# The closing of a nearest-neighbour upsampling kernel: GpSimd in place of SyncE waits for the last transfers, with both closing barriers gathered ahead of that wait

## The chip, the cores and the metric

The kernel runs on one core of one Trainium2 chip. The time is the device time of one execution in microseconds (us). So the time follows that last update, and what comes after the span counts in it. All runs quoted are at a granted clock of 1.0.

Names: VectorE (DVE), ScalarE (ACT), GpSimd (POOL), TensorE (PE) and SyncE (SP) are the five engines. The traces list each engine's waits and semaphore updates under its own queue (SPq, POOLq), called its sequencer here. A semaphore stands in them as a count that instructions and transfers change and on which instructions wait. A transfer counts its landing on one in sixteen increments (256 landing updates for the 16 transfers, in the trace before). "The landing" below means the sixteenth increment of the last store. The "span" runs from the first to the last instruction of the program. The "runtime's close" is the name here for what comes after it, seen only by its semaphore updates.

## The reference

```python
def setup_inputs():
    return {'x': np.random.randn(16, 64, 64, 64).astype(np.float32), 'scale_factor': 2}

def reference(x, scale_factor):
    # ... result[:, :, i, j] = x[:, :, i // scale_factor, j // scale_factor]
```

A pure copy: 16.78 MB are read and each element is written four times, 67.11 MB.

## The kernel before

Four loads of 4 MB bring the input into one large tile. VectorE and ScalarE expand pieces of it (9/16 and 7/16 of the rows), and SyncE issues twelve stores. The first eight are of 4 MB and the last four of 8 MB.

```python
def store(part, r0, k, at):
    # ... kv = k * 9 // 16; u is a piece of the big tile, seen as rows to be expanded
    nc.vector.tensor_copy(out=u[:, :kv], in_=expanded(xp[:, r0 : r0 + kv, :]))
    nc.scalar.copy(out=u[:, kv:], in_=expanded(xp[:, r0 + kv : r0 + k, :]))
    # ...
    nc.sync.dma_start(out=dst[:, r0 : r0 + k, :], in_=u)
# ...
for n, (q, r0) in enumerate(small):
    store(q, r0, 32, WX + n % 2 * (WU // 2))
for n, (q, r0) in enumerate(large):
    store(q, r0, 64, (0, WX)[n % 2])
```

The change concerns what the framework puts behind this. It stands in no line of the kernel; the profile puts it down to one line, L138 before, called the closing line here. It gathers the engines at two barriers, 0 and 1: each engine reports its arrival to GpSimd, which releases all when they have come. As built, the closing block is this (my shortening; "arrive" is a DRAIN that adds 1 to the gather semaphore, "pass" waits for the release semaphore and takes 1 off it):

```
SyncE:                       wait for the 8 semaphores of all 16 transfers and for both copy engines
                             (5 event-semaphore instructions and a DRAIN), then
                             arrive 0, pass 0, arrive 1, pass 1
ScalarE, VectorE, TensorE:   arrive 0, pass 0, arrive 1, pass 1
GpSimd:                      DRAIN d0, gather 0 (wait for 4 arrivals), release 0 (+4),
                             DRAIN d1, clear (semaphores 99 to 108 to zero), DRAIN d2,
                             gather 1, release 1
```

Of the kernel before, what the change touches and what calls it, by code (L numbers as in the profile page):

```python
# [1 line left out]

# [4 lines left out]



EARLY = 1  # L10


def begin_before_barrier(nc):



    blocks = nc.main_func.blocks
    main, body = blocks[0], blocks[1]
    sp = mybir.EngineType.SP
    loads = [i for i in body.instructions if i.engine == sp][:EARLY]  # L20
    for load in loads:
        assert isinstance(load, mybir.InstDMACopy), type(load)
        assert not (load.sync_info and load.sync_info.on_wait)
    names = [i.name for i in loads]
    body.instructions = [i for i in body.instructions if i.name not in names]
    kept = list(main.instructions)
    at = next(
        n
        for n, i in enumerate(kept)
        if i.engine == sp and isinstance(i, mybir.InstDrain)  # L30
    )
    kept[at:at] = loads
    main.instructions = kept


@with_exitstack
def kernel(
    ctx: ExitStack,
    tc: tile.TileContext,
    x: bass.AP,  # L40
    scale_factor: int,
    out: bass.AP,
):
    nc = tc.nc
    nc.at_finalize(begin_before_barrier)
    P = nc.NUM_PARTITIONS
    s = int(scale_factor)
    B, C, H, W = x.shape
    R = B * C * H
    fdt = x.dtype  # L50



    WX = R // P * W
    WU = 16384
    mem_pool = ctx.enter_context(tc.tile_pool(name="mem", bufs=1))
    mem = mem_pool.tile([P, WX + WU], fdt, name="mem")



    M4 = R // (4 * P)
    blocks = [(1, M4, 0), (1, M4, 2), (1, M4, 3), (4, M4 // 4, 1)]
    WB = M4 * W
    assert M4 * P * 4 == R and 2 * WB == WU

    xf = x.rearrange("b c h w -> (b c h) w")
    of = out.rearrange("b c (h hd) w -> (b c h) (hd w)", hd=s)

    parts = []
    for n, (j, m, slot) in enumerate(blocks):  # L70
        first = n * P * M4
        xt = mem[:, slot * WB : (slot + 1) * WB].rearrange(
            "p (j m w) -> p j m w", j=j, m=m
        )
        nc.sync.dma_start(
            out=xt.rearrange("p j m w -> p j (m w)"),
            in_=xf[first : first + P * M4, :].rearrange(
                "(j p m) w -> p j (m w)", j=j, p=P
            ),
        )  # L80
        parts.append([(xt[:, jj], first + jj * P * m, m) for jj in range(j)])

    def expanded(rows):
        return rows.unsqueeze(2).unsqueeze(4).to_broadcast(
            [P, rows.shape[1], s, W, s]
        )

    def store(part, r0, k, at):

        xp, first, m = part  # L90
        kv = k * 9 // 16
        u = mem[:, at : at + k * s * W * s].rearrange(
            "p (k a w b) -> p k a w b", k=k, a=s, w=W
        )
        nc.vector.tensor_copy(out=u[:, :kv], in_=expanded(xp[:, r0 : r0 + kv, :]))  # L95
        nc.scalar.copy(out=u[:, kv:], in_=expanded(xp[:, r0 + kv : r0 + k, :]))  # L96
        dst = of[first : first + P * m, :].rearrange("(p m) w -> p m w", p=P)
        nc.sync.dma_start(out=dst[:, r0 : r0 + k, :], in_=u)



    small = [(q, r0) for n in (0, 3) for q in parts[n] for r0 in range(0, q[2], 32)]
    large = [(q, r0) for n in (1, 2) for q in parts[n] for r0 in range(0, q[2], 64)]
# [6 lines that stand above are left out]
# [1 line left out]
_INS = ['x', 'scale_factor']  # L111
_OUTS = [((16, 64, 128, 128), 'float32')]

_NUMBERS = {'scale_factor': 2}


# [26 lines left out]
```

## Time and profile before

| | before |
|---|---|
| time, median of 3 runs | 199.46 us (199.43 to 199.73) |
| span of the profiled execution | 197.712 us |
| share of the 16 DMA engines in use | 98.9% |
| VectorE, ScalarE busy | 20%, 26% |
| last store issued / landed | 164.576 / 196.899 us |
| landing to end of span | 0.813 us |
| end of span to last semaphore update of the runtime's close | 1.907 us |

From the profile page of the kernel before, the busy shares, the DMA queue's line and the chain of waits:

```profile
DVE 40.2 (20%) x12; ACT 51.3 (26%) x13; POOL 0.2 (0%) x4
q1 hardware_dynamic: 2688, 83.89, 98.9%
DMA 69%; ACT 14%; issue 0%; ACTq 0%
```

The transfers fill the whole span (98.9%). No change in the waits at the end can move that part. What follows the last landing is invisible in these shares, because semaphore instructions are not counted as busy. It has to be read from the closing line's own instructions.

The view of the closing line's instructions, kernel before. The columns are: line, engine's queue, operation, count, shortest/median/longest duration in ns, first and last start in us:

```profile
L138 SPq EVENT_SEMAPHORE  x7: 17/28/28, 165.0 to 197.7; - x7
L138 POOLq EVENT_SEMAPHORE  x4: 17/17/17, 197.1 to 197.6; - x4
L138 POOLq DRAIN  x3: 34/41/70, 0.8 to 197.5; - x3
L138 SPq DRAIN  x3: 7/7/7, 197.0 to 197.3; - x3
L138 PEldq EVENT_SEMAPHORE  x2: 51/51/51, 197.2 to 197.7; - x2
L138 POOLq EVENT_SEMAPHORE_RANGE_CLEAR  x1: 93/93/93, 197.3 to 197.3; - x1
```

All four gathers and releases of GpSimd lie at 197.1 us or later, and so does the clear. Its first DRAIN, d0, ran at 0.8 us. Whom SyncE's queue waited for (total us, times, longest):

```profile
SPq L138 <- DMA out_dram<-mem: 31.8, 2, 19.3
```

The trace's instruction records resolve the tail to the nanosecond (start, duration in ns; the passes of ScalarE and VectorE and the arrivals are left out; S97 is the release semaphore, S96 the gather):

```
196.899      sixteenth increment of the last store (S108)
196.916  28  SyncE   wait S108, S102 ends
196.981   7  SyncE   DRAIN (last of the waits)
197.039   7  SyncE   DRAIN, arrive 0
197.071  17  GpSimd  gather 0
197.149  17  GpSimd  release 0
197.230  70  GpSimd  DRAIN
197.329  93  GpSimd  clear
197.451  34  GpSimd  DRAIN
197.529  17  GpSimd  gather 1
197.607  17  GpSimd  release 1
197.661  51  TensorE pass 1        -> span ends 197.712
```

Each of these starts after the one above it, so all 0.813 us are on the critical path, although they are 0.4% of the time.

### The profile page before, as it was taken

The page shows a single profiled execution, that of the slowest core. Times are in us where ns is not written, and L with a number is a line of the kernel's source. Part 1 is how long each engine was busy: PE and PEld are TensorE (multiplying, and loading weights), DVE is VectorE, ACT ScalarE, POOL GpSimd, SP SyncE. Part 2 cuts the span into 40 slices and gives each one's busy share as a digit, 9 for nine tenths or more (in the row PEclk, how much of TensorE's full clock was granted, in tenths as well). Part 3 has the DMA queues.
Part 4 walks back from the last instruction along what each step waited for, and adds up shares of the span by engine and source line. Part 5 has one row for each costly group of instructions (what it writes and reads, how often), then busy time and mean ns, then how long its engine had stood idle before and what let it go on. Part 6 is the DMA issues. An engine that isn't in the chain of part 4 may idle for free.

```text
span 197.7 us, 116 instructions
## 1 busy us (share of the span) xinstructions
DVE 40.2 (20%) x12; ACT 51.3 (26%) x13; POOL 0.2 (0%) x4
## 2 busy tenths in 40 slices
DVE  0055000000405059505050007200810090000000
ACT  2057000000415150606069207400830092000000
POOL 0000000000000000000000000000000000000000
DMA  8999999999999999999999999999999999999994
GB/s 318 424 424 424 438 464 383 424 413 424 424 424 424 444 444 451 451 424 438 424 424 424 424 424 424 464 477 491 451 451 424 424 424 424 424 424 424 424 424 212
DMA packets 2688, 83.89 MB, mean 424 GB/s; under 512 B 256, under 2 KB 256, under 8 KB 256
## 3 DMA queue, kind: packets, MB, share of 16 engines
q1 hardware_dynamic: 2688, 83.89, 98.9%
HBM read 16.78 MB, written 67.11 MB: 424 GB/s over the span
## 4 chain that ended last, share of the span: by engine, by line
DMA 69%; ACT 14%; issue 0%; ACTq 0%
DMA out_dram<-mem 63%; ACT mem L96 14%; DMA mem<-in_x_dram 6%; ACTq L96 0%
## 5 line engine op out<-in xcount | busy, mean ns | idle before, releaser
L96 ACT COPY mem<-mem 128x3584 f32<-128x3584 f32 (+1 forms) x12 | 50.0, 4174 | 112.5 <-DMA out_dram<-mem 102.2
L95 DVE COPY mem<-mem 128x4608 f32<-128x4608 f32 (+1 forms) x12 | 40.2, 3359 | 123.1 <-DMA out_dram<-mem 110.8
L96 ACT ACT_TABLE_LOAD x1 | 1.3, 1283 | 0.8 <-PEq L124 0.8
L124 POOL MEMSET const-bfloat16-1.0<- 128x1 bf16 x1 | 0.1, 102 | 0.0
L124 POOL MEMSET const-uint8-127<- 128x1 uint8 x1 | 0.1, 102 | 0.0
L124 POOL MEMSET const-float32-0.0<- 128x1 f32 x1 | 0.1, 99 | 0.2 <-issue 0.2
L124 POOL MEMSET const-float32-1.0<- 128x1 f32 x1 | 0.1, 99 | 0.0
## 6 DMA issues: line engine op xcount, KB each, us to landing
out_dram<-mem SPq DMA_DIRECT2D x8, 4096.0 KB, 16.1
mem<-in_x_dram SPq DMA_DIRECT2D x4, 4096.0 KB, 25.8
out_dram<-mem SPq DMA_DIRECT2D x4, 32.3
```

Source lines behind the costliest of these rows:

```text
L95: nc.vector.tensor_copy(out=u[:, :kv], in_=expanded(xp[:, r0 : r0 + kv, :]))
L96: nc.scalar.copy(out=u[:, kv:], in_=expanded(xp[:, r0 + kv : r0 + k, :]))
L124: nc = _bacc.Bacc("TRN2", target_bir_lowering=False, num_devices=1)
```

## The change

Its intent: do all closing work that does not need the data while the last transfer is still under way. GpSimd, which has to perform the clear and the release anyway, waits for the transfers itself, so that no hand-over from SyncE is left behind the landing. Both gathers and the first release move ahead of that wait. The waits are sorted so that the last store's semaphore is the last to be waited for. The diff without its assertions:

```diff
+def close_on_gpsimd(nc):
+    # ...  last = semaphore of the last store; mine = GpSimd's instructions of the closing block
+    wait = end[0]                       # SyncE's DRAIN with all the waits
+    waits = sorted(wait.sync_info.on_wait, key=lambda w: w.id != last)
+    d0, gather0, release0, d1, clear, d2, gather1, release1 = mine
+    landed = mybir.InstDrain(
+        name=wait.name, engine=pool, debug=wait.debug,
+        sync_info=mybir.SyncInfo(on_wait=waits, on_update=[]),
+    )
+    others = [i for i in end if i.engine != pool and i is not wait]
+    blocks[-1].instructions = others + [
+        d0, gather0, release0, gather1, d1, landed, clear, d2, release1
+    ]
 # ...
     nc.at_finalize(begin_before_barrier)
+    nc.at_finalize(close_on_gpsimd)
```

Putting `last` first in the list looks odd. The waits stand in five event-semaphore instructions, with one wait left on the DRAIN itself, which executes last. In the changed kernel that one is S108, the first of the sorted list. In the kernel before, whose list is not sorted, it is S101 (196.981), and the last store's semaphore (S108) stands in the last of the five event-semaphore instructions (196.916), with one DRAIN behind it.

More of the change, by code (lines that the diff above doesn't have):

```diff
@@ L33, in begin_before_barrier @@
     main.instructions = kept
+def close_on_gpsimd(nc):
+    blocks = nc.main_func.blocks
+    sp, pool = mybir.EngineType.SP, mybir.EngineType.Pool
+    stores = [
+        i
+        for i in blocks[1].instructions
+        if i.engine == sp and isinstance(i, mybir.InstDMACopy)
+    ]
+    last = stores[-1].sync_info.on_update[0].id
+    end = list(blocks[-1].instructions)
+    wait = end[0]
+    assert wait.engine == sp and isinstance(wait, mybir.InstDrain)
+    waits = sorted(wait.sync_info.on_wait, key=lambda w: w.id != last)
+    assert waits[0].id == last and len(waits) > 2
+    mine = [i for i in end if i.engine == pool]
+    kinds = [type(i).__name__ for i in mine]
+    assert kinds == [
+        "InstDrain",
+        "InstEventSemaphore",
+        "InstEventSemaphore",
+        "InstDrain",
+        "InstISA",
+        "InstDrain",
+        "InstEventSemaphore",
+        "InstEventSemaphore",
+    ], kinds
+    d0, gather0, release0, d1, clear, d2, gather1, release1 = mine
+    landed = mybir.InstDrain(
+        name=wait.name,
+        engine=pool,
+        debug=wait.debug,
+        sync_info=mybir.SyncInfo(on_wait=waits, on_update=[]),
[3 more added lines that the diff above has]
+        d0, gather0, release0, gather1, d1, landed, clear, d2, release1
+    ]
 @with_exitstack
```

## The prediction

> **What bounds the kernel now.** The kernel moves 83.89 MB (16.78 read, 67.11 written) and the page's queue table gives the transfers 98.9% of 16 engines' span; VectorE and ScalarE are busy 20% and 26%. The chain of waits puts 69% on DMA and 14% on ScalarE's copies, the last transfer being a 32 us store issued at 164.58 us. The change touches none of that. It only touches what follows the last landing.
>
> **The tail before** (the trace's instruction records and semaphore updates; the view of the closing line's instructions gives their first and last starts and durations). The sixteenth increment of the last store comes at 196.899 us. SyncE's wait ends 17 ns later (196.916); its closing DRAINs start at 196.981 and 197.039. GpSimd, the gatherer, then runs in series: gather 197.071, release 197.149, DRAIN 197.230, semaphore clear 197.329 (93 ns), DRAIN 197.451, gather 197.529, release 197.607. The last engine (PE) passes at 197.661 and takes 51 ns: span 197.712. So 0.81 us lies between the last landing and the end of the span, all of it on the critical path.
>
> **What the change does.** The order of instructions shows the compute and transfer parts identical. In the closing block all four other engines arrive at both barriers, and GpSimd does gather 0, release 0, gather 1 and a DRAIN, as soon as the last store is issued (about 165 to 165.5 us), under the 32 us transfer: free. The early landings are waited for there too; the last store's own semaphore is put by the lowering on the final DRAIN, so nothing but that one wait is left to end when the data lands. After it there is: DRAIN, clear, DRAIN, release, and the engines' pass. Number of instructions: unchanged.
>
> **Cost, with before's own steps.** Wake 17 ns (as SyncE; GpSimd woke from its gather 25 ns after its last increment, so the same size), DRAIN to clear 99, clear to DRAIN 122, DRAIN to the next instruction 78, release to PE's pass 54, pass 51: 0.42 us after landing in place of 0.81. [...] Saved: 0.39 us (SyncE's two DRAINs and hand-over 0.155; first gather and release, 0.159; second gather 0.078). All of it is critical, since nothing runs beside it.
>
> **What lies outside the span.** 199.46 - 197.71 = 1.75 us. After the span the semaphore updates go on to 199.62 us[...]. It starts from the same last release in both kernels, so I expect it to shift whole. It might gain or lose 0.1 to 0.2 us because four engines now stand at their last wait for 32 us.
>
> **Prediction.** 199.46 - 0.39 = 199.07 us, that is 0.2% faster; range 198.85 to 199.28 (the three runs before spread over 0.30). Chance of faster by over 2%: 0.005; within 2%: 0.99; slower by over 2%: 0.005.
>
> **What would show each step.** Span of about 197.3 us; the closing line's SyncE records with no wait for a landing; GpSimd's gathers near 165 us; the clear about 0.12 us after the last landing and the final release about 0.32 after; last store's issue still near 164.6 and its landing near 196.9; DMA share still 99%. Wrong if: GpSimd wakes from a landing clearly later than SyncE; the clear takes longer right after the wait; a gather is still found after the landing; the transfers' own time changes; or the runtime's close takes up the gain because an engine other than the releasing one limits it (then the span falls by 0.39 and the time by less).

The steps, each from the start of one record to the start of the next in the trace before, are 17 + 99 + 122 + 78 + 54 + 51 = 421 ns left after the landing; of 813 ns that saves 0.392 us, and 199.46 - 0.39 = 199.07 us. In "What lies outside the span", "it" is what follows the span; that it would shift whole, and the 0.1 to 0.2 us allowed for, were guesses.

## The result, and the profile after

| | before | changed |
|---|---|---|
| median time, same rounds | 199.56 us (6 runs) | 199.08 us (6 runs; 198.94 to 199.31) |
| span of the profiled execution | 197.712 | 197.279 |
| last store issued / landed | 164.576 / 196.899 | 164.547 / 196.902 |
| landing to end of span | 0.813 | 0.377 |
| end of span to last update of the close | 1.907 | 1.905 |

The ratio is 0.9977, with a 95% interval of 0.9964 to 0.9990. Ratios and intervals are those of the record, from the fast runs of the same rounds; they are not quite the ratio of the medians, nor always that of the plain means (0.9994 in e2, where the record has 0.9997). The kernel is faster by 0.2%, well inside "same" at the 2% mark.

From the profile page of the changed kernel, the same three lines; they show no change in the body beyond 0.2 points of DMA share:

```profile
DVE 40.2 (20%) x12; ACT 51.3 (26%) x13; POOL 0.2 (0%) x4
q1 hardware_dynamic: 2688, 83.89, 99.1%
DMA 69%; ACT 14%; issue 0%; ACTq 0%
```

The closing line's instructions in the changed kernel (columns as before):

```profile
L183 POOLq EVENT_SEMAPHORE  x9: 17/17/43, 165.1 to 197.2; - x9
L183 POOLq DRAIN  x4: 34/38/70, 0.8 to 197.1; - x4
L183 SPq DRAIN  x2: 7/68/128, 164.9 to 165.3; - x2
L183 SPq EVENT_SEMAPHORE  x2: 17/17/17, 165.2 to 197.2; - x2
L183 PEldq EVENT_SEMAPHORE  x2: 51/51/51, 165.2 to 197.2; - x2
L183 POOLq EVENT_SEMAPHORE_RANGE_CLEAR  x1: 93/93/93, 197.0 to 197.0; - x1
```

GpSimd now has nine event-semaphore instructions in place of four, five of them the waits that SyncE had; the first starts at 165.1 us. SyncE's DRAINs are over by 165.3 us. In SyncE's waits the landing is gone from the closing line; what it waits for there is the barrier (the profile puts it down to another engine's queue, PE's):

```profile
SPq L183 <- PEq L183: 32.1, 2, 31.9
```

The tail in the changed kernel's instruction records:

```
165.084  17  GpSimd  gather 0
165.163  17  GpSimd  release 0
165.412  17  GpSimd  gather 1
165.493  70  GpSimd  DRAIN
   ...
196.902      sixteenth increment of the last store (S108)
196.925  34  GpSimd  DRAIN, wait S108 ends
196.989  93  GpSimd  clear
197.110  34  GpSimd  DRAIN
197.174  17  GpSimd  release 1
197.228  51  TensorE pass 1        -> span ends 197.279
```

Start to start the steps are 23 + 64 + 121 + 64 + 54 + 51 = 377 ns. Before they were 17 + 65 + 58 + 32 + 78 + 81 + 99 + 122 + 78 + 78 + 54 + 51 = 813 ns. The difference, 0.436 us, is the gain. By these steps SyncE's arrival and the hand-over are 0.090 of it, the first gather and release 0.159, the second gather 0.092, the DRAIN ahead of the clear 0.035, and SyncE's step from its wait to its DRAIN, which the sorting removed, 0.065; the wake is 0.006 longer.

### The profile page after: what moved, and what is told of

Its sections match the earlier page's. It is cut to its first block, busy times and chain, and to the rows that moved or that the text cites. A ratio compares the mean times of both kernels' runs of the same rounds, so it can differ in the third digit from the quotient of the medians.

```text
span 197.3 us, 116 instructions
## 1 busy us (share of the span) xinstructions
DVE 40.2 (20%) x12; ACT 51.3 (26%) x13; POOL 0.2 (0%) x4
## 3 DMA queue, kind: packets, MB, share of 16 engines
q1 hardware_dynamic: 2688, 83.89, 99.1%
## 4 chain that ended last, share of the span: by engine, by line
DMA 69%; ACT 14%; issue 0%; ACTq 0%
DMA out_dram<-mem 63%; ACT mem L141 14%; DMA mem<-in_x_dram 6%; ACTq L141 0%
```

## The experiments

Two theories were held against each other at first. **Theory A**: the gain is the number of serial closing steps that still have to run after the landing; which engine waits hardly matters. **Rival B**: GpSimd is simply the better engine to see the landing. A second pair came up later. **Theory D**: the runtime's close, which follows the span and lies in the measured time, is a chain through the engines in a fixed order, and how fast the last waiter leaves the program is part of the time. Its rival: that close follows the end of the span by a constant.

All edits are to the changed kernel's list of closing instructions, so e1 and e2 have the sorted waits as well. From the third on (but not in e9, the changed kernel itself), two things are used. The clear covers only semaphores 99 to 107, and the last store's own semaphore is set back by the instruction that waits for it:

```python
rest = [w for w in waits if w.id != last]        # the nine other waits
clear = mybir.InstISA(..., ant_dict=dict(old, range_last=last - 1))   # 99..107
def landed_and_reset(engine):                    # wait for the last store, then take 32 off again
    return mybir.InstEventSemaphore(name="I-50000", engine=engine, ...,
        sync_info=mybir.SyncInfo(on_wait=[waits[0]], on_update=[  # update_mode "sem-sub-imm"
            mybir.SyncUpdate(id=last, update_value=waits[0].wait_value, ...)]))
```

All kernels gave correct results. e1 to e4 ran on one chip in shared rounds (kernel before: 199.44 us there, 9 runs), e5 to e8 on a second (199.51 us, 9 runs), e9 to e11 on a third (199.57 us, 11 runs).

### e1: only the engine

```diff
-        d0, gather0, release0, gather1, d1, landed, clear, d2, release1
+        landed, d0, gather0, release0, d1, clear, d2, gather1, release1
```

> Only the waiting engine is changed: GpSimd instead of SyncE waits for the transfers, and both closing barriers follow that wait as in the kernel before. Theory A (the gain is the number of serial closing steps left after the last landing; the engine hardly matters): SyncE's two DRAINs and the hand-over (0.155 us) are replaced by GpSimd's own two DRAINs (about 0.13 to 0.14); end of span 0.79 us after the last landing (0.813 before, 0.377 in the changed kernel); time within 0.05 us of the kernel before, about 199.5. Rival B (GpSimd is the better engine to see the landing): most of the 0.44 us comes, end of span at 0.40 to 0.55 after the landing, time about 199.15 to 199.25.

Measured: 199.48 us, ratio 1.000 (0.9987 to 1.0012); landing to end of span 0.811 us. Theory A had said 0.79, rival B 0.40 to 0.55. GpSimd waking (24 ns after the landing) and its own DRAINs take as long as SyncE's DRAINs and the hand-over did. GpSimd sees the landing no earlier than SyncE: its wait ended 23 or 24 ns after it in every trace, SyncE's 16 or 17. In the traces of the kernel before and of the changed kernel the closing DRAINs last 34 to 70 ns on GpSimd and 7 to 19 ns on the other engines, apart from those right behind a copy or a store; those that GpSimd executes after the last store's issue take 64 to 114 ns from start to start. Rival B falls: this edit is worth 0.002 us.

```profile
L173 POOLq EVENT_SEMAPHORE  x9: 17/17/5069, 110.0 to 197.6; - x9
L173 POOLq DRAIN  x4: 34/38/70, 196.9 to 197.5; - x4
```

The second line shows that the edit did one thing more: all four of GpSimd's DRAINs in the closing line (the wait for the last store is one) now follow the landing, also d0, which ran at 0.8 us before. It takes 0.078 us from start to start there. With d0 left ahead, the engine alone would have gained about 0.08 us; that is an estimate from these steps, which was not run, and still far from rival B's figure.

### e2: only the order

```diff
-    landed on GpSimd; GpSimd: d0, gather0, release0, gather1, d1, landed, clear, d2, release1
+    SyncE:  arrive 0, pass 0, landed, arrive 1, pass 1
+    GpSimd: d0, gather0, release0, gather1, d1, clear, d2, release1
```

> Only the order is changed: SyncE still waits for the transfers, but after it has passed the first barrier, so that barrier 0 and four of the five arrivals of barrier 1 are done under the last transfer. Theory A: after the landing there are SyncE's DRAIN and its arrival, GpSimd's gather 1, DRAIN, clear, DRAIN, release, pass: with the steps of before 0.017+0.058+0.032+0.081+0.10+0.122+0.078+0.054+0.051 = 0.59 us from landing to end of span, 0.22 us less than before, time about 199.3. Rival B (the engine is what matters): no gain, 0.81 us and about 199.5.

Measured: landing to end of span 0.578 us in the trace (theory A: 0.59). The time does not settle it: median 199.32 us against 199.44, but with one run of 199.80 the ratio is 0.9997 (0.9984 to 1.0011). Taken from the trace, the order gives 0.235 us, of which 0.064 is the sorted wait (0.076 us from the landing to SyncE's arrival, for 0.140 before). In the closing line SyncE's last DRAIN starts at 196.9 us, and GpSimd's first gather already at 165.0:

```profile
L176 SPq DRAIN  x3: 7/7/129, 164.8 to 196.9; - x3
L176 POOLq EVENT_SEMAPHORE  x4: 17/17/17, 165.0 to 197.3; - x4
```

So the two halves, as edited, do not add: engine 0.002, order 0.235, both together 0.436. The engine's part, worth almost nothing in e1, is worth 0.201 us once the gathers are out of the way (0.578 less 0.377). Only then are SyncE's arrival, GpSimd's gather and the DRAIN after it the hops that remain between landing and clear. So Theory A holds as a count of steps. That the engine hardly matters is true of how it sees the landing, not of the steps it leaves behind.

### e3: the last store waited for first

```diff
-        d0, gather0, release0, gather1, d1, landed, clear, d2, release1
+        d0, gather0, release0, gather1, d1, landed_and_reset(pool), landed_on(pool, rest),
+        clear, d2, release1
```

> The changed kernel, with the wait for the last store put ahead of the waits for the nine others, which are then all satisfied but still have to be executed (four event-semaphore instructions at about 0.087 us each, as they stand in the changed kernel's trace, and 0.066 for the first). Theory A: 0.066 + 4 x 0.087 = 0.41 us more than the changed kernel after the landing, 0.79 us to end of span, the time back at about 199.5 although all barriers are gathered ahead. If satisfied waits cost nothing, 0.38 us and about 199.1.

Measured: 199.47 us, ratio 1.000 (0.9988 to 1.0013); landing to end of span 0.824 us (expected 0.79). Four waits for semaphores that had long reached their value started at 197.076, 197.168, 197.254 and 197.341 us, then the DRAIN at 197.428. A satisfied wait for two semaphores thus cost GpSimd 0.086 to 0.092 us from start to start. The wait for the last store, here an instruction of its own, takes 0.096 us to the next one, where 0.066 had been expected. GpSimd's last closing instructions in e3:

```profile
L212 POOLq EVENT_SEMAPHORE  x9: 17/17/43, 165.1 to 197.7; - x9
L212 POOLq EVENT_SEMAPHORE_RANGE_CLEAR  x1: 92/92/92, 197.5 to 197.5; - x1
```

The wrong order of the waits thus cost as much as the whole change gains (0.447 us, 0.824 less 0.377, against 0.436). This is the worst order, though, and not what the sorting gained. In the framework's own order the last store's semaphore has a single DRAIN behind it, 0.065 us on SyncE before; on GpSimd it would be about 0.09, an estimate from the steps here. No run has the change without the sorting.

### e4: the clear as well goes ahead of the landing

```diff
-        d0, gather0, release0, gather1, d1, landed, clear, d2, release1
+        d0, gather0, release0, gather1, d1, landed_on(pool, rest), clear, d2,
+        landed_and_reset(pool), release1
```

> The changed kernel going further: the range clear covers only the nine other semaphores and runs before the last landing; the last store's own semaphore is set back by the wait instruction itself, followed at once by the release. Theory A: 0.023 + 0.07 + 0.054 + 0.051 = 0.20 us from landing to end of span (0.377 in the changed kernel), time 0.18 us below the changed kernel, about 198.9. If something outside the span limits (the runtime's close), the span falls but the last semaphore update after it does not.

Measured: 198.88 us, ratio 0.9971 (0.9959 to 0.9984). The closing line's clear and the last DRAIN of GpSimd in this kernel:

```profile
L212 POOLq DRAIN  x4: 34/38/70, 0.7 to 178.0; - x4
L212 POOLq EVENT_SEMAPHORE_RANGE_CLEAR  x1: 92/92/92, 177.9 to 177.9; - x1
```

The clear has moved from 197.0 to 177.9 us, behind the landing of the store before the last. Landing to end of span is 0.207 us (expected 0.20), and the last update of the close is 2.111 us after the landing, 0.171 less than in the changed kernel. Nothing outside the span took it back.

### e5 to e8 and e11: one engine alone waits for the last store

Up to here the last update of the runtime's close came 1.904 to 1.907 us after the end of the span in all six traces. After the span, semaphore 2 is updated in two rounds of nine; each update is called a hop here. In every one of the six, the third hop of the first round came 0.205 us after the second, where the others of the first five are 0.02 to 0.04 apart. The second round takes 0.357 or 0.358 us from first to last update, with steps of 0.023 to 0.047 and one of 0.10 after the fifth, called the turn here. Only the first round is longer, by the late third hop: 0.525 us in the changed kernel, whose rounds end 0.760 and 1.905 us after the span. That each of the first five hops stands for one engine leaving the program, in a fixed order with GpSimd third, was the guess at this point (the expectations below speak of a closing barrier and of a chain); the runs test it. So here everything including the final release was done ahead, and a single engine waited:

```diff
-        landed_and_reset(pool), release1
+        release1, landed_and_reset(pool)    # e5; e6: (sp), e7: (ScalarE), e8: (TensorE), e11: (VectorE)
```

> All of the kernel's own closing steps run under the last transfer, the final release too: the other four engines leave at about 178 us; GpSimd alone waits for the last store and sets its semaphore back in the same instruction. In every trace so far the closing barrier that follows the span (updates of semaphore 2[...]) has its third hop 0.205 us after the second where 0.04 is usual, and that third hop comes 0.579 us after GpSimd's last release. Theory D (a fixed chain of engines, GpSimd is the third, and its own leaving of the program limits): span ends 0.04 us after the landing, first two hops already at about 178 us, third hop 0.60 after the landing, last update 2.03 after it (2.28 in the changed kernel, 2.11 in e4): time 0.25 us below the changed kernel, about 198.8. Rival (the close follows the end of the span by 1.905 us whatever engine ends it, as in all six traces so far): last update 1.95 after the landing, about 198.75, with no hop before the span's end.

> As e5, but SyncE is the engine that waits alone for the last store. Theory D with SyncE as the fifth and last of the chain: the first four hops lie at about 178 us and the fifth comes 0.3 us after the landing if SyncE leaves as fast as the first engine of the chain does (0.286 us from its pass), 0.6 if as slowly as GpSimd; last update 1.364 us after the fifth hop, that is 1.67 to 1.96 after the landing (2.28 in the changed kernel): time 0.3 to 0.6 us below the changed kernel, 198.45 to 198.8, and below e5. Rival (the close follows the span's end by 1.905 us): last update 1.95 us after the landing, equal to e5. So the engine would matter after all, but for how it leaves, not for how it sees the landing.

> As e5, but ScalarE waits alone. Theory D with ScalarE second in the chain: hop one at about 178 us, hop two 0.3 to 0.33 us after the landing, three more hops of 0.04, 0.04, 0.02, then 1.364: last update about 1.78 to 1.81 after the landing, time about 0.48 us below the changed kernel, 198.6; slower than e6 if SyncE leaves as fast, since three hops remain.

> As e5, but TensorE waits alone. Theory D with TensorE first in the chain: no hop before the landing, the first 0.29 to 0.31 us after it, then 0.034, 0.038, 0.044, 0.023 and 1.364: last update about 1.79 to 1.82 after the landing, time about 0.47 us below the changed kernel, 198.6. The third hop's gap, 0.205 us in all kernels where GpSimd is released last, falls to about 0.04, because GpSimd has left long before.

> As e5, but VectorE waits alone. The chain of hops was SyncE fifth, ScalarE second, TensorE first, GpSimd third; VectorE is left for the fourth place: three hops at about 178 us, the fourth 0.16 to 0.3 us after the landing (ScalarE took 0.16 from its wait's end, TensorE 0.33), the fifth 0.023 later, the last update 1.36 after that: 1.55 to 1.7 us after the landing, between e6 (1.48) and e8 (1.86), time about 198.4 to 198.6.

Measured, all from the traces but the last three columns; us. The times of e11 are of another chip, where e6's kernel took 198.22. "Leaving" is from the start of the record of the engine's last wait to the first hop that comes after the landing:

| run, waiter | landing to end of span | hops of the first round before the landing | leaving | landing to last update | median time | ratio | interval |
|---|---|---|---|---|---|---|---|
| e5 GpSimd | 0.041 | 2 | 0.579 | 2.034 | 198.74 | 0.9962 | 0.9949 to 0.9974 |
| e8 TensorE | 0.079 | 0 | 0.326 | 1.857 | 198.66 | 0.9957 | 0.9944 to 0.9971 |
| e7 ScalarE | 0.039 | 1 | 0.156 | 1.647 | 198.49 | 0.9948 | 0.9935 to 0.9960 |
| e11 VectorE | 0.049 | 3 | 0.203 | 1.619 | 198.42 | 0.9939 | 0.9924 to 0.9955 |
| e6 SyncE | 0.034 | 4 | 0.158 | 1.484 | 198.36 | 0.9944 | 0.9932 to 0.9957 |

The updates of semaphore 2 relative to the landing, first round, from the traces' semaphore updates:

```
changed  +0.612  +0.646  +0.851  +0.895  +0.918  | +1.017 +1.056 +1.090 +1.137
e5      -18.610 -18.576  +0.603  +0.646  +0.669  | +0.769 +0.807 +0.841 +0.888
e6      -18.607 -18.573 -18.368 -18.324  +0.175  | +0.219 +0.257 +0.291 +0.339
e7      -18.618  +0.178  +0.216  +0.260  +0.284  | +0.382 +0.421 +0.455 +0.502
e8       +0.354  +0.388  +0.426  +0.471  +0.494  | +0.592 +0.631 +0.666 +0.712
e11     -18.610 -18.576 -18.371  +0.231  +0.255  | +0.354 +0.392 +0.426 +0.473
```

The order is read off directly: TensorE first, ScalarE second, GpSimd third, VectorE fourth, SyncE fifth. Theory D holds and the constant of 1.905 us falls: in e5 the last update came 1.993 us after the end of the span, in e6 1.450. GpSimd is the slowest to leave: 0.579 us from its last record in e5, and the same 0.579 from its last release to the third hop in the changed kernel. With GpSimd gone early, the third hop follows the second by 0.038 us in e7 and e8, so the 0.205 was GpSimd coming late. My expectations took 0.3 us for leaving where nothing was known: SyncE and ScalarE turned out twice as fast (e6 0.19 us below the low end of what was expected, e7 0.13 below), TensorE a little slower (e8 0.04 above). In e6, 0.055 of the 0.19 is the turn: with SyncE last to come it took 0.044 us (0.045 in e10) in place of 0.098 or 0.099, and the last update followed the fifth hop by 1.309 in place of 1.364. ScalarE leaves as fast as SyncE (0.156 and 0.158 us), but three hops and the longer turn follow it, so e6 is the fastest.

The end of the span misleads here. e5, e6 and e7 all end their span 0.034 to 0.041 us after the landing, yet the last updates of e5 and e6 lie 0.55 us apart. The closing line in e5, two lines, and in e6, four:

```profile
L212 POOLq EVENT_SEMAPHORE  x9: 17/17/43, 165.1 to 196.9; - x9
L212 SPq EVENT_SEMAPHORE  x2: 17/17/17, 165.2 to 178.0; - x2
```

```profile
L212 POOLq EVENT_SEMAPHORE  x8: 17/30/43, 165.3 to 178.2; - x8
L212 SPq EVENT_SEMAPHORE  x3: 17/17/17, 165.4 to 197.2; - x3
L212 PEldq EVENT_SEMAPHORE  x2: 51/51/51, 165.4 to 178.2; - x2
L212 POOLq EVENT_SEMAPHORE_RANGE_CLEAR  x1: 92/92/92, 178.0 to 178.0; - x1
```

In e6 only one instruction of the closing, SyncE's third event semaphore, is left at 197.2 us; all others are done by 178.2. SyncE's waits in e6 show that one wait for the last landing, from 178.2 to 197.15 us; the profile names SyncE's own queue, which issued the store:

```profile
SPq L212 <- SPq L212: 18.9, 1, 18.9
```

### e9 and e10: the changed kernel and e6 side by side

> The changed kernel itself, on the same chip and in the same rounds as e10 and e11, for a direct comparison. Theory A and D: 0.377 us from landing to end of span and 2.28 to the last update, as in its first trace; about 0.44 us below the kernel before.

> The kernel of e6 again (SyncE alone waits for the last store, everything else done under it): last update 1.48 us after the landing; 1.24 us below the kernel before and 0.80 below e9, by the traces so far. If the gain of e6 was luck of its chip or rounds, it comes out nearer to e9.

Measured in the same rounds on one chip: before 199.57 us, changed kernel 199.13 (ratio to before 0.9971, 0.9956 to 0.9986), e6's kernel 198.22 (0.9928, 0.9913 to 0.9942). Landing to last update: 2.282 and 1.477 us, the same as in their first traces to within 0.01. So SyncE waiting alone beats both kernels: 0.7% below the kernel before, and 0.45% below the changed one (mean 198.25 over mean 199.15). That is 0.90 us by the times against 0.805 by the traces. The times are the looser measure here: the kernel before had two late runs in these rounds (199.94 and 200.48), and the kernels' own runs spread over 0.26 to 0.29. The traces show spread ahead of the tail: over the thirteen of them the last store was issued between 164.45 and 164.81 us, whereas the time from its issue to its landing varied by 0.035 us only.

What stays open: why GpSimd takes 0.58 us to leave, what the sorting alone is worth, and whether some other runtime would object to four engines leaving the program while the last store is still on its way. In these runs the runtime's first round of hops was not completed before the waiting engine had come, and the results were right.

## Why the prediction was right

The prediction said 199.07 us (198.85 to 199.28) and "same"; 199.08 was measured, and 199.13 in the repeat. That the time was met to 0.01 us is luck: the start was 199.46, the median of three runs, where six gave 199.56, and the saving was put at 0.39 where the medians differ by 0.48 and the traces by 0.436. The two errors cancel. "Same" was safe as well, since the whole tail is 0.4% of the time. The mechanism is tested by the steps in the traces. Point by point:

- **The body is untouched, the tail is serial.** Right. The last store's issue and landing moved by 0.03 and 0.003 us, and the DMA share is 99.1%. e1 to e4 each changed the tail by what their count of steps said, to within 0.04 us.
- **0.42 us left after the landing, 0.39 saved.** The mechanism held and the sum was a little off: 0.377 left, 0.436 saved. The mis-sized terms were "DRAIN to clear 99", which measured 64 ns, and "DRAIN to the next instruction 78", which measured 64. I had taken both from steps of another context. The 99 belonged to a DRAIN of 70 ns just after a release; the one that waits for the landing takes 34 ns. The wake took 23 ns, for 17 estimated. So the clear came 0.087 us after the landing (0.12 said) and the last release 0.272 after it (0.32 said).
- **Start to start counts what the records leave out.** Counting each step from the start of one record to the start of the next served well. The hand-over from release to TensorE's pass was 54 ns in both traces, of which the release's record shows 17. Nor is the waiting in the record of the wait for the last store: it starts 17 ns after the landing in the trace before and 23 ns after it in the changed one, where the instruction ahead of it started at 177.615 and 177.621 us.
- **The split of the gain into "SyncE's two DRAINs and hand-over 0.155, first gather and release 0.159, second gather 0.078".** As a sum it nearly came out (0.392 for 0.436); as shares of the two halves of the change it would have misled. e1 gained 0.002 us where the first share was 0.155, because GpSimd's own DRAINs took the place of SyncE's, d0 among them, which need not have stood there. Of that share 0.065 came from the sorting. e2 shows 0.235 for the order with the sorting.
- **The runtime's close shifts whole.** Right for this change: 1.907 and 1.905 us from span's end to last update, and the 0.1 to 0.2 us that I allowed for did not appear. The reason I gave ("the same last release in both kernels") fits too: the third hop came 0.579 us after GpSimd's last release in both traces. When other engines end the program, it does not shift whole (1.450 in e6, 1.993 in e5).

What I had not seen is that a wrong order of the waits cost 0.4 us (e3: 0.824 us from landing to end of span, for 0.377), and that GpSimd, good for the clear, was the worst engine to be the last one out (e5 against e6: last update 2.034 and 1.484 us after the landing).

## What to carry to other kernels

What ran after the last landing here was a serial chain of sequencer instructions, at 0.032 to 0.122 us from start to start in the kernel before: count them, move ahead whatever needs no data, and let the wait that ends last be the last one executed, since even a satisfied wait cost 0.086 to 0.092 us on GpSimd (e3). Halves of such a change need not add, because what one half leaves standing can hide the other's worth (0.002 and 0.235 us here, for 0.436 together); test each alone, and look in its trace for what else the edit moved. Choose the engine that leaves last by how soon the runtime's own close can go on behind it, and read that from the semaphore updates after the span, not from the end of the span (e5 and e6 end their spans 0.041 and 0.034 us after the landing, their last updates come 2.034 and 1.484 us after it).
